# A two-layer trunk on one core: activation sums made a block ahead, own buffers for decay rows, and other places for the first weights

## The chip, the core and the metric

The kernel runs on one core of one Trainium2 chip. Its engines work side by side, each on a queue of its own and in the queue's order: TensorE (PE) multiplies into eight accumulator banks, VectorE (DVE) and ScalarE (ACT) work element by element, GpSimd (POOL) does a few small steps and issues some transfers, and SyncE (SP) issues the transfers of weights. The metric is the time of one execution on the device in microseconds (us).

## The reference

The input x has 256 tokens of width 2048, in float32. Layer 0 multiplies the normed x with one wide matrix (l0_w_in), whose columns feed an mLSTM group (q, k, v, output gate o, gates i and f) and a state-space group (z, x, B, C, dt); both results go side by side through l0_w_out. Layer 1 is causal attention with 16 heads and rotary positions; with 256 tokens, one block is all there is. Each layer ends with a gated feed-forward network (FFN) of inner width 5632. Cut to its core:

```python
for layer in range(2):
    xn = rms_norm(x, norm_mix[layer])
    if layer == 0:
        q, k, v, o, ig, fg, z, xbc, dt = split(xn @ w_in)
        hm = rms_norm(mlstm_chunkwise(q, k, v, ig, fg)) * sigmoid(o)
        xs, bm, cm = split(silu(causal_depthwise_conv(xbc)))
        y = ssd_chunked(xs, dt, a, bm, cm) + ssd_d * xs
        y = rms_norm_by_group(y * silu(z))
        x = x + concatenate([hm, y]) @ w_out
    else:
        x = x + moba_attention(rope(q), rope(k), v) @ w_o     # q, k, v = split(xn @ w_qkv)
    xn = rms_norm(x, norm_ffn[layer])
    x = x + (silu(xn @ w_gate) * (xn @ w_up)) @ w_down
out = rms_norm(x, final_norm)
```

## The kernel before

**Numbers in two parts.** Each float32 operand is split into a high part in a reduced format (the cast, on ACT: names ending in h, such as wh) and the low rest (a subtraction on DVE: wl). A product is three matmuls: high by high, high by low, low by high. So each weight tile costs a transfer into `raw`, an ACT cast (L410, in the projections L335) and a DVE subtraction (L412, L336) before PE can use it.

**Units.** In the z block, l0_w_out, the FFN and l1_w_o, `block` works on two strips of 512 columns at a time and goes through the depth of 2048 in eight units of 256 rows. A unit is of kind P, plain, with 24 matmuls of 128x512, or of kind S, summed: a Strassen-like step with 21 matmuls, that multiplies sums of weight tiles (`sums`, L419 to L423, on DVE) with sums of activation tiles (`skx`). PLAN_X is "PSPSPSPP", PLAN_LATE "PPPSPSPP", PLAN_O "PPPPPSPP". An S unit adds into four banks acc_f and four banks acc_e; behind the last S unit the four acc_e are added up (`pre`, L475 to L479). Most blocks come in two halves (q = 0 and 1) of two strips each.

**Sums of activations.** `sums_of(kt, j)` (L293 to L300) makes one set: xg, high plus low part (L299), four combinations sf (L283 to L286), then the split of sf into skx: an ACT cast (L196) and a DVE subtraction (L197). `block` asks for them at most three units ahead of their use, within its own half. Sets live in three buffers, tag `small`.

**Turns.** Activations must lie with the depth on the partitions, so results are turned by PE (p_tr, L253), four 128x128 pieces into a bank, and then split by ACT and DVE (L196 and L197, or L199 and L200 with gains), in `turned`. `later(wait, ...)` puts a turn, or another small step, a number of units behind. The split of a turn is marked with a priority of 1200, which lets the scheduler place it ahead of other work on ACT and DVE.

**Order.** Each engine executes its instructions in the order in which the scheduler put them; a waiting instruction holds up everything behind it on that engine.

**Stages.** The first 529 us hold the projections of layer 0 by strips (`lin_w`, `lin_a`: accumulators acc_w, acc_a), with the gates at 110 to 135 us. In between stand mLSTM heads and state-space heads; each needs decay rows: `decay_rows` has POOL issue two transfers from a scratch tensor (L654), and DVE adds masks to them (L658). Their buffer is the one `rows`, or one of four `ba`, which the mLSTM also uses. From 532 us the z block runs, in two halves; behind each, y is gated: thz (ACT L914, DVE L915), y (DVE L916), sums of squares (ACT L505), rs (DVE L191), rrg (POOL L192), y again (ACT L925), for four 128x512 pieces. From 640 us l0_w_out multiplies the mLSTM part (`mixed`, tiles mx) in two halves, and from 742 us the state-space part (`gated`, tiles my). Then the first FFN (to 1540), q, k, v and attention in four groups (to 1835), l1_w_o (`add_blocks` on oT) and the second FFN.

**Start of the kernel.** The sums of squares of x (ACT L505) write their squares into a temporary buffer; from them the norm is made (`row_norm`: dg on DVE L315, p_rb on PE L316). The gate weights wg come by POOL's queue and are cast by ACT (L196).

**Banks.** `ring["acc"]` is (0, 1, 2, 3, 4, 5); accumulators are taken in turn. In the last attention group (g = 3), the values' acc_a are set to start at bank 4, which the keys' strip used last.

Of the kernel before, what the change touches and what calls it, by code (L numbers as in the profile page):

```python
# [17 lines left out]
P = 128  # L18
# [23 lines left out]
STAGING = {"raw": 3, "wh": 3, "wl": 3}  # L42
MIXER = ({"raw": 4, "wh": 3, "wl": 3}, {"cb": 1}, {"rows": 1}, {"gap": 12288}, {"hm": 2}, {"gap": 192}, {"ba": 4}, {"cols": 2},
         {"wide": 2})
# [21 lines left out]
def hybrid_trunk(ctx: ExitStack, tc: tile.TileContext, a: dict, out: bass.AP):  # L66
# [42 lines left out]
    def open_staging():  # L109

        close_stage()
        for guard, pool, tags in open_pool("st", (STAGING,)):
            ctx.callback(guard.__exit__, None, None, None)
            staging.append((pool, tags))

    def held_tile(tag, shape, name, dt=F32):
# [3 lines left out]
        raise KeyError(tag)  # L120

# [125 lines left out]
    def transpose_split(kt, b, src, gcol, half):  # L247
# [6 lines left out]
        with tc.high_priority(offset=1200):  # L254
            turned(kt, b, pt.rearrange("p (a b) -> p a b", a=2), gcol, half)
# [65 lines left out]
    def chunks(w, col, nk, first=KC):  # L321

        n = 4 if staging else KC
        for k in range(0, nk, KC):
            if k % n == 0:
                raw = held_tile("raw", [P, n, STRIP], "raw")
                wh = held_tile("wh", [P, n, STRIP], "wh", F32R)
                wl = held_tile("wl", [P, n, STRIP], "wl", F32R)
# [65 lines left out]
    def weights(src, row, summed):  # L394

        def unit(kind, name, dt=F32):
            turn[kind] = turn.get(kind, -1) + 1
            spare = kind == "raw" and turn[kind] % 4 == 3
            return held_tile("rawx" if spare and stage["spare"] else kind, [P, 4, STRIP], name, dt)

        raw = unit("raw", "raw")
# [4 lines left out]
        def parts(of, cuts):  # L406
            h = unit("wh", "wh", F32R)
            l = unit("wl", "wl", F32R)
# [6 lines left out]
        with tc.high_priority(offset=800):  # L415
            if not summed:
                return parts(raw, (slice(0, 2), slice(2, 4)))
            sums = unit("raw", "sums")
# [6 lines left out]
    def block(src, kt, row, nk, plan, after_sums=None, lead=1, pairs=None):  # L425
# [21 lines left out]
        for i_, j in enumerate(order):  # L447
            for i in range(i_, min(i_ + 3, n)):
# [54 lines left out]
    def sumsq(acc, src):  # L503
        j = t2([P, src.shape[-1]], "sq")
# [25 lines left out]
    for c in range(4):  # L530
        for t in range(NT):
            sumsq(ss0[:, t, c:c + 1], xin[t][:, c * STRIP:(c + 1) * STRIP])
# [263 lines left out]
    def ssd_half(s, half):  # L796
        need("cb")
        h0 = 8 * s + 4 * half
        srows = decay_rows(MH + h0, slot_b if s > 1 and half else slot_a)
# [50 lines left out]
    def add_blocks(w, kt, row, nk, plans, finish=None, begin=None, whole=None, pairs=None):  # L850

        for q in range(2):
# [11 lines left out]
            F, _ = block(((w, c0), (w, c0 + STRIP)), kt, row, nk, plans[q], add_all, 2 if final else 1, pairs and list(pairs))  # L864
# [282 lines left out]
```

## Time and profile before

| what | value |
|---|---|
| runs | 2668.72, 2671.80 and 2671.93 us, median 2671.8 us |
| profiled execution | 2667.37 us, its span 2665.5 us |
| PE, DVE, ACT busy | 97%, 82%, 54% of the span |
| granted clock of PE, mean | 0.99 |
| HBM read | 492.39 MB, 186 GB/s over the span |

A row of the waits says which engine and line waited, for whom, for how long in total, how many times, and the longest. A row of stretches gives the busy time of each engine between two points, and the clock that PE was granted. A row of the order of time gives start, length, engine, line, operation, and in brackets how long the engine had been idle and what ended that.

### The profile page before, as it was taken

Reading aid. Unit: us, or ns where it says so; the run is one execution under the profiler, and the core shown is the slowest. Engines: PE = TensorE matmul, PEld = TensorE weight load, DVE = VectorE, ACT = ScalarE, POOL = GpSimd, SP = SyncE. Lnnn points to the kernel's source line nnn. Section 1 sums busy time; section 2 is a strip of 40 time slices with the busy share of each in tenths; the row PEclk is TensorE's granted clock in tenths of the full one; section 3 lists DMA queues with packets and bytes.
Section 4 is the critical chain, followed back from the end, with each engine's and each line's share of the span. In section 5 each row is a group of like instructions: output and inputs, shape, how many; then the busy total and the mean of one; then the engine's idle time right before and its main releaser. Section 6 shows DMA issues by size and latency. Waiting matters only on the chain.

```text
span 2665.5 us, 32524 instructions
## 1 busy us (share of the span) xinstructions
PE 2595.1 (97%) x12201; PEld 2137.3 (80%) x12201; DVE 2172.7 (82%) x2784; ACT 1442.8 (54%) x1916; POOL 46.0 (2%) x81
## 2 busy tenths in 40 slices
PE   8999999988999999999999999999999999999997
PEld 7888878866878777878787888887787788778876
DVE  5676777788999998889889975665899888988897
ACT  5465655556556555455445555555565545554544
POOL 2000010000000000000000000000000000000000
PEclk9999999998999999999999999999999999999999
DMA  7566576453656466556655655554546565566564
GB/s 215 169 190 197 165 218 186 143 197 127 221 170 216 159 210 215 177 187 200 211 190 190 196 184 183 177 173 131 189 167 213 173 214 182 197 199 196 190 199 140
DMA packets 254767, 496.68 MB, mean 186 GB/s; under 512 B 15704, under 2 KB 16608, under 8 KB 254352
## 3 DMA queue, kind: packets, MB, share of 16 engines
q1 hardware_dynamic: 250528, 483.52, 55.8%
q0 software_dynamic: 2896, 8.51, 1.1%
q10 hardware_dynamic: 1184, 2.56, 0.3%
q8 instruction: 96, 1.57, 0.2%
q14 instruction: 63, 0.52, 0.1%
HBM read 492.39 MB, written 2.14 MB: 186 GB/s over the span
## 4 chain that ended last, share of the span: by engine, by line
PE 86%; DVE 7%; ACT 3%; DMA 2%; issue 2%; POOL 0%; SPq 0%; DVEq 0%; POOLq 0%; ACTq 0%
PE acc_f L441 16%; PE acc_f L442 16%; PE acc_f L440 15%; PE acc_w L351 10%; PE acc_w L355 5%; PE acc_e L441 3%; PE acc_e L440 3%; PE acc_e L442 3%; PE acc_a L378 3%; PE acc_a L380 3%; PE acc_a L379 3%; DVE wl L412 3%; ACT wh L410 1%; PE p_tr L253 1%; PE p_y L823 1%
## 5 line engine op out<-in xcount | busy, mean ns | idle before, releaser
L410 ACT CAST wh<-raw 128x1024 fp32r<-128x1024 f32 (+1 forms) x548 | 599.7, 1135 | 443.8 <-PE acc_f L442 319.9
L412 DVE TENSOR_TENSOR wl<-raw,wh 128x1024 fp32r<-128x1024 f32 (+1 forms) x548 | 713.3, 1325 | 129.6 <-ACT wh L410 126.5
L336 DVE TENSOR_TENSOR wl<-raw,wh 128x1024 fp32r<-128x1024 f32 (+1 forms) x257 | 309.0, 1218 | 175.5 <-ACT wh L335 174.7
L441 PE MATMUL acc_f<-wl,x 128*128 128x512 f32 x1024 | 401.0, 392 | 0.5
L440 PE MATMUL acc_f<-wh,x 128*128 128x512 f32 x1024 | 399.9, 392 | 0.0
L442 PE MATMUL acc_f<-wh,x 128*128 128x512 f32 x1024 | 399.3, 390 | 0.0
L335 ACT CAST wh<-raw 128x1024 fp32r<-128x1024 f32 (+1 forms) x257 | 264.0, 1046 | 223.8 <-PE acc_w L351 134.8
L410 ACT CAST wh<-sums 128x1024 fp32r<-128x1024 f32 x216 | 221.6, 1048 | 184.0 <-PE acc_f L442 91.1
L412 DVE TENSOR_TENSOR wl<-sums,wh 128x1024 fp32r<-128x1024 f32 x216 | 259.0, 1220 | 12.1 <-ACT wh L410 11.9
L441 PEld LDWEIGHTS acc_f<-wl,x 128*128 128x128 f32 x1024 | 192.3, 188 | 43.2 <-DVE wl L412 2.7
L440 PEld LDWEIGHTS acc_f<-wh,x 128*128 128x128 f32 x1024 | 192.3, 188 | 43.1 <-ACT wh L410 4.1
L442 PEld LDWEIGHTS acc_f<-wh,x 128*128 128x128 f32 x1024 | 192.3, 188 | 39.2
L351 PE MATMUL acc_w<-xa,wh 128*128 128x512 f32 x768 | 211.0, 403 | 1.6 <-ACT wh L335 1.6
L351 PEld LDWEIGHTS acc_w<-xa,wh 128*128 128x128 f32 x768 | 140.6, 191 | 28.3 <-ACT wh L335 2.0
L351 PE MATMUL acc_w<-x,wh 128*128 128x512 f32 x512 | 138.6, 399 | 0.0
L419 DVE TENSOR_TENSOR sums<-raw 128x1024 f32<-128x1024 f32 x108 | 131.8, 1220 | 5.0 <-DMA raw<-in_l_ffn_up 2.5
L355 PE MATMUL acc_w<-xa,wl 128*128 128x256 f32 x768 | 122.4, 284 | 0.0
L355 PEld LDWEIGHTS acc_w<-xa,wl 128*128 128x128 f32 x768 | 111.1, 192 | 6.9
L441 PE MATMUL acc_f<-wl,ha 128*128 128x512 f32 x280 | 109.5, 393 | 1.2 <-DVE wl L412 0.9
L441 PE MATMUL acc_f<-wl,hb 128*128 128x512 f32 x280 | 109.7, 393 | 0.9 <-DVE wl L412 0.6
L442 PE MATMUL acc_f<-wh,hb 128*128 128x512 f32 x280 | 108.7, 389 | 0.0
L442 PE MATMUL acc_f<-wh,ha 128*128 128x512 f32 x280 | 108.5, 389 | 0.0
(363 smaller groups left out, 4750.0 us busy)
## 6 DMA issues: line engine op xcount, KB each, us to landing
raw<-in_l_w_in SPq DMA_DIRECT2D x191, 512.0 KB, 3.8
raw<-in_l_ffn_gate SPq DMA_DIRECT2D x176, 512.0 KB, 3.9
raw<-in_l_ffn_up SPq DMA_DIRECT2D x176, 512.0 KB, 4.9
raw<-in_l_ffn_down SPq DMA_DIRECT2D x176, 512.0 KB, 5.1
raw<-in_l_w_qkv SPq DMA_DIRECT2D x96, 512.0 KB, 4.5
raw<-in_l_w_out SPq DMA_DIRECT2D x64, 512.0 KB, 5.2
raw<-in_l_w_o SPq DMA_DIRECT2D x32, 512.0 KB, 4.9
rows<-scr POOLq DMA_DIRECT2D x10, 512.0 KB, 5.6
```

Of the source, the lines that this page charges most:

```text
L335: nc.scalar.copy(wh[:, ks, :], raw[:, ks, :])
L336: nc.vector.tensor_sub(wl[:, ks, :], raw[:, ks, :], wh[:, ks, :].bitcast(F32))
L351: nc.tensor.matmul(banks[f], wh[:, kk, f * P:(f + 1) * P], kt.both(k0 + kk), start=k0 + kk == 0, stop=False, skip_group_check=True)
L355: nc.tensor.matmul(banks[f][:, :T], wl[:, kk, f * P:(f + 1) * P], kt.parts(k0 + kk)[0], start=False, stop=k0 + kk == nk - 1, skip_group_ch ...
L378: nc.tensor.matmul(banks[t], xh[:, ts], wh[:, kk, :], start=k0 + kk == 0, stop=False)
L379: nc.tensor.matmul(banks[t], xh[:, ts], wl[:, kk, :], start=False, stop=False)
L410: nc.scalar.copy(h[:, c, :], of[:, c, :])
L412: nc.vector.tensor_sub(l[:, c, :], of[:, c, :], h[:, c, :].bitcast(F32))
L419: nc.vector.tensor_sub(sums[:, 0:2, :], raw[:, 2:4, :], raw[:, 3:0:-2, :])
L440: nc.tensor.matmul(dst, ah, bh, start=start, stop=False)
L441: nc.tensor.matmul(dst, ah, bl, start=False, stop=False)
L442: nc.tensor.matmul(dst, al, bh, start=False, stop=stop)
```

## The change

It has seven pieces; the work done is the same, instruction for instruction, apart from where it stands and where its data lie.

1. `block` and `add_blocks` take a list `ahead`: sets of activation sums of the next half or the next block that are made at a given unit of this one. The z block's first half makes the set that its second half lacks; the second half makes the three of l0_w_out's `mixed`; the second half of `mixed` makes two of `gated`; l1_w_o's first half makes two of its second.
2. The decay rows have three buffers `rows` of their own, in place of one plus 12288 bytes of gap, and no longer use `ba`.
3. The staging buffers for weights are nine pools of one buffer each, in another order of addresses, so that the first unit of z lies over space that is free by then.
4. Only the turns for the normed x of later stages (x1, x2, x3) keep the priority of 1200; the turns of mixed, gated, oT and h have 0.
5. The last attention group takes its banks in the order 0, 1, 4, 5, 2, 3, from the first one.
6. The squares of x go into the tile kT, which is written later.
7. The norm for the rotary table comes one step later.

```diff
-STAGING = {"raw": 3, "wh": 3, "wl": 3}
-MIXER = ({"raw": 4, "wh": 3, "wl": 3}, {"cb": 1}, {"rows": 1}, {"gap": 12288}, {"hm": 2}, {"gap": 192}, {"ba": 4}, {"cols": 2},
-         {"wide": 2})
+STAGING = tuple({tag: 1} for tag in "raw1 raw2 wh1 wh2 wl1 raw0 wh0 wl0 wl2".split())
+MIXER = ({"raw": 4, "wh": 3, "wl": 3}, {"cb": 1}, {"rows": 3}, {"hm": 2}, {"gap": 192}, {"ba": 4}, {"cols": 2}, {"wide": 2})
...
+    def unit(kind, shape, name, dt=F32):
+
+        if not staging:
+            return held_tile(kind, shape, name, dt)
+        n = turn[kind] = turn.get(kind, -1) + 1
+        if kind == "raw" and stage["spare"]:
+            if n % 4 == 3:
+                return held_tile("rawx", shape, name, dt)
+            n -= n // 4
+        return held_tile(f"{kind}{n % 3}", shape, name, dt)
...
-        with tc.high_priority(offset=1200):
+        with tc.high_priority(offset=1200 if kt.name in ("x1", "x2", "x3") else 0):
             turned(kt, b, pt.rearrange("p (a b) -> p a b", a=2), gcol, half)
...
-    def block(src, kt, row, nk, plan, after_sums=None, lead=1, pairs=None):
+    def block(src, kt, row, nk, plan, after_sums=None, lead=1, pairs=None, ahead=()):
...
         for i_, j in enumerate(order):
+            for i, kt_, j_ in ahead:
+                if i == i_:
+                    sums_of(kt_, j_)
             for i in range(i_, min(i_ + 3, n)):
                 if plan[i] == "S" and order[i] not in kt.sums:
                     sums_of(kt, order[i])
...
-            sumsq(ss0[:, t, c:c + 1], xin[t][:, c * STRIP:(c + 1) * STRIP])
+            sumsq(ss0[:, t, c:c + 1], xin[t][:, c * STRIP:(c + 1) * STRIP], kT[:, 2 * c:2 * c + 2, :].rearrange("p a b -> p (a b)"))
...
-        srows = decay_rows(MH + h0, slot_b if s > 1 and half else slot_a)
+        srows = decay_rows(MH + h0, slot_b)
...
-        F, pre = block(tuple((w_in, C_Z + (s0 + n) * STRIP) for n in range(2)), xt0, 0, KD, PLAN_X if q else PLAN_LATE)
+        F, pre = block(tuple((w_in, C_Z + (s0 + n) * STRIP) for n in range(2)), xt0, 0, KD, PLAN_X if q else PLAN_LATE,
+                       ahead=((4, mixed, 1), (6, mixed, 3), (7, mixed, 5)) if q else ((4, xt0, 1),))
...
-    add_blocks(a["l0_w_out"], mixed, 0, KD, (PLAN_X, PLAN_X))
+    add_blocks(a["l0_w_out"], mixed, 0, KD, (PLAN_X, PLAN_X), ahead=((), ((2, gated, 3), (4, gated, 1))))
...
-    later(5, "rope", rope_norm)
+    later(6, "rope", rope_norm)
...
     for g in range(4):
+        if g == 3:
+            ring["acc"], turn["acc"] = (0, 1, 4, 5, 2, 3), 0
         q = rope_strip(g * STRIP, "q4")
         k = rope_strip(D + g * STRIP, "k4")
-        if g == 3:
-            turn["acc"] = 4
...
-    add_blocks(a["l1_w_o"], oT, 0, KD, (PLAN_O, PLAN_X), finish)
+    add_blocks(a["l1_w_o"], oT, 0, KD, (PLAN_O, PLAN_X), finish, ahead=(((6, oT, 1), (7, oT, 3)), ()))
```

The changed kernel's lines stand 10 to 13 further down: L299 is L309 there, L412 is L418, L916 is L928.

The order of DVE's instructions behind the first half of z, before (xa_148 is the first tile of the normed x, y_2730 and y_2731 the two token halves of y):

```order
L915 SCALAR_TENSOR_TENSOR thz<-thz,pre 128x512
L916 SCALAR_TENSOR_TENSOR y_2730<-thz,rh_426,y_2730 128x512
L191 TENSOR_SCALAR rs<-ssg 128x2
L915 SCALAR_TENSOR_TENSOR thz<-thz,pre 128x512
L916 SCALAR_TENSOR_TENSOR y_2731<-thz,rh_426,y_2731 128x512
L299 TENSOR_TENSOR xg<-xa_148 128x512
L191 TENSOR_SCALAR rs<-ssg 128x2
L283 TENSOR_TENSOR sf<-xg 128x128
```

and the same set of sums in the changed kernel, whose tile is named xa_144, in the first half of z:

```order
L309 TENSOR_TENSOR xg<-xa_252 128x512
L296 TENSOR_TENSOR sf<-xg,sf 128x128
L293 TENSOR_TENSOR sf<-xg 128x128
L294 TENSOR_TENSOR sf<-xg 128x128
L295 TENSOR_TENSOR sf<-sf,xg 128x128
L309 TENSOR_TENSOR xg<-xa_144 128x512
L207 TENSOR_TENSOR skx<-sf,skx 128x4x128
L418 TENSOR_TENSOR wl<-raw,wh 128x1024
```

The set has moved from behind the gating of y to the first half's own two sets.

DVE at the change from z to l0_w_out, before (mx_3802 and mx_4292 are tiles of `mixed`):

```order
L916 SCALAR_TENSOR_TENSOR y_2730<-thz,rh_426,y_2730 128x512
L191 TENSOR_SCALAR rs<-ssg 128x2
L915 SCALAR_TENSOR_TENSOR thz<-thz,pre 128x512
L916 SCALAR_TENSOR_TENSOR y_2731<-thz,rh_426,y_2731 128x512
L299 TENSOR_TENSOR xg<-mx_3802 128x512
L191 TENSOR_SCALAR rs<-ssg 128x2
```

and in the changed kernel (my_5772 is a tile of `gated`, whose turns are L210):

```order
L294 TENSOR_TENSOR sf<-xg 128x128
L295 TENSOR_TENSOR sf<-sf,xg 128x128
L210 SCALAR_TENSOR_TENSOR my_5772<-p_tr,pv,my_5772 128x256
L296 TENSOR_TENSOR sf<-xg,sf 128x128
L927 SCALAR_TENSOR_TENSOR thz<-thz,pre 128x512
L418 TENSOR_TENSOR wl<-raw,wh 128x1024 x2
L418 TENSOR_TENSOR wl<-raw,wh 128x1536
L207 TENSOR_TENSOR skx<-sf,skx 128x4x128 x2
L928 SCALAR_TENSOR_TENSOR y_2718<-thz,rh_414,y_2718 128x512
L210 SCALAR_TENSOR_TENSOR my_5772<-p_tr,pv,my_5772 128x256
```

The sums of `mixed` now stand ahead of the gating or behind its first step, and turns and weights stand among its steps.

PE in the last attention group, before (p_o is the previous heads' output, p_pt the turn of the probabilities, acc_a the values' accumulators):

```order
L1028 MATMUL p_qk<-k_14167,q_13933 128x128
L1029 MATMUL p_qk<-k_14167,q_13933 128x256
L1059 MATMUL p_o<-pT,v_14344 128x256
L1060 MATMUL p_o<-pT,v_14344 128x128
L1051 MATMUL p_pt<-ident,prob 128x128
L378 MATMUL acc_a<-wh,x_12269 128x512
```

and in the changed kernel, where p_o comes behind 12 matmuls of acc_a and p_pt behind 48:

```order
L1040 MATMUL p_qk<-k_14178,q_13944 128x128
L1041 MATMUL p_qk<-k_14178,q_13944 128x256
L388 MATMUL acc_a<-wh,x_12280 128x512
L389 MATMUL acc_a<-wl,x_12280 128x512
L390 MATMUL acc_a<-wh,x_12280 128x512
```

The turn of the probabilities no longer stands ahead of the values' matmuls.

More of the change, by code (lines that the diff above doesn't have):

```diff
@@ L111, in open_staging @@
         close_stage()
-        for guard, pool, tags in open_pool("st", (STAGING,)):
+        for guard, pool, tags in open_pool("st", STAGING):
             ctx.callback(guard.__exit__, None, None, None)
@@ L325, in chunks @@
             if k % n == 0:
-                raw = held_tile("raw", [P, n, STRIP], "raw")
-                wh = held_tile("wh", [P, n, STRIP], "wh", F32R)
-                wl = held_tile("wl", [P, n, STRIP], "wl", F32R)
+                raw = unit("raw", [P, n, STRIP], "raw")
+                wh = unit("wh", [P, n, STRIP], "wh", F32R)
+                wl = unit("wl", [P, n, STRIP], "wl", F32R)
             step = KC if k else first
@@ L394, in weights @@
     def weights(src, row, summed):
[L396 to L401, printed above, removed]
+        shape = [P, 4, STRIP]
+        raw = unit("raw", shape, "raw")
         for i, (w, col) in enumerate(src):
@@ L406, in parts @@
         def parts(of, cuts):
-            h = unit("wh", "wh", F32R)
-            l = unit("wl", "wl", F32R)
+            h = unit("wh", shape, "wh", F32R)
+            l = unit("wl", shape, "wl", F32R)
             for c in cuts:
@@ L417, in weights @@
                 return parts(raw, (slice(0, 2), slice(2, 4)))
-            sums = unit("raw", "sums")
+            sums = unit("raw", shape, "sums")
             nc.vector.tensor_sub(sums[:, 0:2, :], raw[:, 2:4, :], raw[:, 3:0:-2, :])
@@ L501, in block, with sumsq @@
         return F, pre
-    def sumsq(acc, src):
-        j = t2([P, src.shape[-1]], "sq")
+    def sumsq(acc, src, j=None):
+        j = t2([P, src.shape[-1]], "sq") if j is None else j
         nc.scalar.activation(j, src, AF.Square, accum_out=acc)
@@ L848, in col_norm, with add_blocks @@
         return r
-    def add_blocks(w, kt, row, nk, plans, finish=None, begin=None, whole=None, pairs=None):
+    def add_blocks(w, kt, row, nk, plans, finish=None, begin=None, whole=None, pairs=None, ahead=((), ())):
         for q in range(2):
@@ L863, in add_blocks @@
             final = q and whole is not None
-            F, _ = block(((w, c0), (w, c0 + STRIP)), kt, row, nk, plans[q], add_all, 2 if final else 1, pairs and list(pairs))
+            F, _ = block(((w, c0), (w, c0 + STRIP)), kt, row, nk, plans[q], add_all, 2 if final else 1, pairs and list(pairs),
+                         ahead[q])
             if final:
```

## The prediction

> **What bounds the kernel now.** I read the page's busy line first, then the waits of TensorE (PE), then a table of stretches around them, and last the order of time inside the long waits.
>
> ```profile
> span 2665.5 us, 32524 instructions
> PE 2595.1 (97%) x12201; PEld 2137.3 (80%) x12201; DVE 2172.7 (82%) x2784; ACT 1442.8 (54%) x1916; POOL 46.0 (2%) x81
> ```
>
> PE is the bound: it sits idle for 2665.5 − 2595.1 = 70.4 us, and its instructions stay the same in number and shape. Only that idle time, and the slow clock that goes with it, can be won. The waits of PE (total us, times, longest us) say whom it waits for:
>
> ```profile
> PE acc_f L440 <- ACT skx L196: 23.6, 4, 10.8
> PE p_pt L1051 <- ACT prob L1045: 6.6, 2, 6.5
> PE acc_e L440 <- ACT wh L410: 4.4, 8, 0.7
> PE p_rb L316 <- DVE dg L315: 4.4, 2, 3.6
> PE acc_f L440 <- ACT wh L410: 3.3, 2, 3.1
> PE p_xs L793 <- DVE xsT L754: 3.1, 1, 3.1
> ```
>
> The table of stretches (width, busy time of PE, PEld, DVE, ACT, POOL, then the granted clock) shows where they lie:
>
> ```profile
> 0.00:45.00 45.00, 35.61 (x181) 29.70 (x182) 25.78 (x45) 27.22 (x53) 14.47 (x36) 0.96 0.75 229
> 360.00:390.00 30.00, 25.71 (x119) 20.48 (x118) 20.98 (x41) 17.53 (x35) 2.13 (x3) 0.94 0.63 206
> 529.00:540.00 11.00, 6.50 (x22) 4.22 (x22) 10.61 (x22) 7.97 (x13) 0.00 (x0) 0.69 0.79 285
> 540.00:585.00 45.00, 45.00 (x200) 37.26 (x199) 37.59 (x39) 21.42 (x21) 0.00 (x0) 1.00 0.55 188
> 585.00:608.00 23.00, 13.36 (x53) 10.38 (x52) 15.14 (x25) 14.76 (x33) 3.15 (x4) 0.78 0.28 92
> 640.00:670.00 30.00, 18.77 (x70) 14.14 (x69) 24.24 (x43) 20.52 (x42) 2.76 (x4) 0.77 0.27 87
> 786.00:800.00 14.00, 12.89 (x56) 10.03 (x55) 10.65 (x15) 7.34 (x7) 0.00 (x0) 1.00 0.52 174
> 925.00:1540.00 615.00, 612.01 (x2693) 493.50 (x2693) 544.36 (x602) 323.90 (x346) 0.00 (x0) 1.00 0.59 194
> 1800.00:1830.00 30.00, 23.55 (x110) 19.64 (x109) 15.61 (x24) 12.79 (x24) 0.00 (x0) 0.89 0.33 106
> 1895.00:1910.00 15.00, 12.69 (x50) 9.89 (x49) 12.07 (x20) 6.63 (x8) 0.00 (x0) 0.89 0.35 112
> 1945.00:2560.00 615.00, 612.79 (x2700) 495.06 (x2698) 544.57 (x612) 318.26 (x334) 0.69 (x1) 1.00 0.59 194
> ```
>
> What a stretch loses I take as its idle time plus (1 − clock) × busy time. Without a stall the clock is 1.00 and a matmul takes 45.00/200 = 0.225 us. So 0–45 loses 9.39 + 1.4 = 10.8; 360–390 loses 5.8; 529–540, the start of the z block, 4.5 + 2.0 = 6.5; 585–608, its second half, 9.64 + 2.9 = 12.6; 640–670, the first half of the l0_w_out block, 11.23 + 4.3 = 15.5; 786–800 1.1; 1800–1830 6.45 + 2.6 = 9.0; 1895–1910 3.7; the two long FFN stretches 3.0 + 2.2 = 5.2.
>
> **The change part by part.** Only what a part's wait costs counts; the work is the same, in another order.
>
> *Sums a block ahead (z second half, l0_w_out, gated, l1_w_o).* The order of time around the wait at 591–601 (start, length, engine, work, in brackets the idle time before it):
>
> ```profile
> 593.18 0.69 POOL L192 TENSOR_TENSOR rrg<-rs,mhalf 128x2 f32<-128x2 f32 x1 [2.02 <-DVE rs L191]
> 593.54 0.69 DVE L915 SCALAR_TENSOR_TENSOR thz<-thz,pre 128x512 f32<-128x512 f32 x1 [0.44 <-ACT thz L914]
> 598.00 0.68 DVE L299 TENSOR_TENSOR xg<-xa 128x512 f32<-128x512 f32 x1
> 600.92 0.60 ACT L196 CAST skx<-sf 128x512 fp32r<-128x512 f32 x1
> 601.58 0.79 PE L440 MATMUL acc_f<-wh,skx 128*128 128x512 f32 x1 [9.64 <-ACT skx L196]
> ```
>
> The sum xg stands in DVE's queue behind four gating steps that pass from ACT to DVE to POOL and back, and PE waits 9.64 us for it. One set of sums is one xg (0.68), four sf and the low part, and the cast of 0.60 on ACT:
>
> ```profile
> L283 DVE TENSOR_TENSOR sf<-xg x30: 278/283/291, 531.3 to 2556.3; 128x128 f32<-128x128 f32 x30
> ```
>
> With 4 × 0.28 and another 0.68 that is about 2.5 us of DVE. That work now runs in the first half, where 540–585 shows 45.00 − 37.59 = 7.4 us of idle DVE: it fits. The gating steps remain, beside unit work whose weights still need DVE, so I do not take all 12.6 but 9 (bounds 3, if DVE passes two thirds of the delay on to the low weights, and 12.6).
>
> In l0_w_out three sets were made after the gating (15.5 lost); now one is made ahead of it and two behind its first step. But the first summed unit of the new block still needs weights whose buffers come free only when the previous block's last unit ends, and DVE has the sums, four additions to the accumulators and the turns of y to do there: by its own rows 24.24 busy of 30. Two 1024-wide low parts, one set of sums and one addition in a row are some 2 × 1.18 + 2.5 + 0.68 = 5.5 us that PE can overtake. I expect a wait of about 5, long enough to keep its slow clock (4.3): 15.5 − 5 − 4.3 = 6.2, taken as 6 (bounds −2, the wait stays and two turns of y come on top, and 15.5). In gated 1 of 1.1 (0 to 1.1); in l1_w_o 2.5 of 3.7 (1 to 3.7), since DVE is busy 12.07 of 15 there and may hand on part of the wait.
>
> A rule weighed here: the Trainium skill's "TensorE: Matmul & The Clock Gate" (Part 1) has the clock drop after at least one idle window of some 3.4 us and return after one busy one. The row 1895–1910 differs: 2.3 us idle in all, clock 0.89. By the page that stretch would lose 2.3 and not 3.7, and the sum would be some 1.4 smaller; by the row it stays.
>
> *First z weights in free space, turns at normal priority.* PE waited 3.1 us for wh at the start of z (the acc_f <- ACT wh row), since ACT's cast stood behind the last work of the strips. With the unit's three buffers in space that is free, transfer and cast come three places earlier, and the eight turns p_tr go behind the unit's 24 matmuls (24 × 0.225 = 5.4 us, which covers tho). I take 5 of 6.5 (2 to 6.5): 1.5 stays because DVE, 10.61 busy of 11, has the second unit's low weights late.
>
> *Three row buffers.*
>
> ```profile
> 135.63 1.57 POOL L654 DMA_DIRECT2D rows<-scr  x2 [1.69 <-PE acc_w L351]
> ...
> 359.25 1.49 POOL L654 DMA_DIRECT2D rows<-scr  x2 [12.92 <-PE p_num L701]
> DVE rows L658 <- DMA rows<-scr: 14.1, 11, 3.8
> rows<-scr POOLq DMA_DIRECT2D x10, 512.0 KB, 5.6
> ```
>
> The transfer at 359.25 waited for a buffer that p_num held; DVE then waited 3.8 us for it, and the 3.1 us of p_xs follow. With own buffers it is issued right behind the early set of 135.63. Of 5.8 lost I take 5 (bounds −3 and 5.8): three sets back to back at 5.6 us a transfer can make DVE wait some 3 us more than it does now around 145, and there only a strip's weight lead covers it.
>
> *Start.*
>
> ```profile
> 34.34 1.48 ACT L196 CAST wgh<-wg 128x1536 fp32r<-128x1536 f32 x1 [5.97 <-DMA wg<-in_l_w_in]
> 11.67 0.47 ACT L199 ACTIVATE xa<-p_tr,pv 128x256 fp32r<-128x256 f32 x1 [1.65 <-PE p_tr L253]
> L558 POOL DMA_DIRECT2D alog<-in_l_ssd_a_log x1: 528/528/528, 7.5 to 7.5; - x1
> ```
>
> The gate cast blocked ACT for 5.97 us and dg behind it (p_rb 3.6). It moves ten places down, and p_rb some 25 matmuls down: 3.6 and its 1.4 of clock come back, 5. Against it the ACT row lam comes up to the tenth place, and waits there for a transfer issued at 7.5; with 5.6 us of landing that is 13.1, against 11.67 when ACT next evacuates a turn now: 1.5 lost. Net 3.5 (1 to 5).
>
> *Bank order of the last attention group.*
>
> ```profile
> 1806.30 2.35 DVE L336 TENSOR_TENSOR wl<-raw,wh 128x1024 fp32r<-128x1024 f32 x2
> 1812.52 0.42 DVE L386 TENSOR_TENSOR rsrc<-acc_w,rsrc 128x256 f32<-128x256 f32 x1
> 1812.90 0.47 PE L1051 MATMUL p_pt<-ident,prob 128*128 128x128 f32 x1 [6.46 <-ACT prob L1045]
> 1813.03 0.77 PE L378 MATMUL acc_a<-wh,x 128*128 128x512 f32 x1
> ```
>
> The 6.46 are put down to prob, yet acc_a starts right behind the accumulator's release at 1812.52 too: two releases end together. Both are dealt with: four banks for acc_a are free, and p_pt goes behind 48 of its matmuls (48 × 0.225 = 10.8 us against 6.46). Weights are there at 1808.65 at the latest. I take 8 of 9.0 (4 to 9).
>
> *FFN and rope.* Six waits of 0.67 (acc_e <- wh) shrink, as wh<-sums comes half a microsecond earlier: 2 of 5.2 (−2 to 5.2). rope's norm goes one step back: 0.5 of p_rb's second wait, 4.4 − 3.6 = 0.8 (0 to 0.8).
>
> Sum: 3.5 + 5 + 5 + 9 + 6 + 1 + 2 + 0.5 + 8 + 2.5 = 42.5. The profiled execution took 2667.4 us, so it becomes 2624.9. The median of the runs, 2671.8, lies 4.4 above it, which I carry over: 2629.
>
> **The rivals.**
> *DVE is the bound from 529 to 830.* In 585–608 it is busy 15.14 of 23, so this stretch waits on a chain; but 529–540 has 10.61 of 11, and 640–670 24.24 of 30, so there its load itself may set the pace. Then the waits only change their name: z start, z second half, l0_w_out and gated give 4 instead of 21, FFN 0 instead of 2. 42.5 − 19 = 23.5 gained: 2648.
> *Everything comes back.* All caps: 5 + 5.8 + 6.5 + 12.6 + 15.5 + 1.1 + 5.2 + 0.8 + 9 + 3.7 = 65; with l0_w_out at 10 still 59.7: 2612. For it speaks that DVE has 18% idle; against it that no DVE work is removed.
> *Slower: late turns.* Turns of mixed, gated, oT and h lose their priority and stand behind weight casts. At eight block halves PE could meet such a turn a whole unit late: 8 × 5.4 = 43 plus the clock (some 2 each, as 585–608 lost 2.9) is 59, which outweighs 42.5: 2688. It decides from 42.5/8 = 5.3 us of lateness on average. In the FFN it cannot:
>
> ```profile
> L197 DVE TENSOR_TENSOR skh<-sf,skh x12: 683/684/686, 884.0 to 2560.6; 128x512 fp32r<-128x512 f32 x12
> L440 PE MATMUL acc_f<-wh,skh x24: 389/389/398, 1003.6 to 2637.0; 128*128 128x512 f32 x24
> ```
>
> The first sum of h is there 119 us before PE reads it, the last 76 us. For the other blocks the order puts the turns two to four rows of weights later (2.4 to 5 us), which their unit order mostly covers.
> *The change does not do what it says.* The new addresses of the first weights may still overlap used space; only the z start hangs on that: 5 less, 2634, inside the forecast.
>
> **How the numbers follow.** Forecast (2620 to 2640) 0.58, DVE as the bound 0.25, everything 0.10, slower 0.05, and 0.02 that every wait only moves and nothing is left. The range, 2611 to 2653, takes in the forecast, the full recovery and most of the DVE case. A measurement here tells some 0.2% (5.3 us) from no change: faster 0.58 + 0.25 + 0.10 = 0.93; of the slower case 0.01 ends within that bound, so same 0.03 and slower 0.04.
>
> **What would show it.** Right: 585–608 without the skx wait, 1800–1830 at clock 1.00 with acc_a ahead of p_pt, no p_xs wait at 375, DVE's longest wait for rows under 2 us, p_rb's wait gone, and a wait of some 5 us for wh, wl or a turn at the head of l0_w_out. Wrong: PE waits of over 5 us for wl or xa, my or p_tr in 585–830 (DVE the bound), a DVE wait for rows at 140–160 with PE idle behind it, ACT waiting for alog for more than 2 us, or a clock under 1.00 in the long FFN stretches.

## The result, and the profile after

The changed kernel took 2628.53 us in the median of four runs (2624.91 to 2630.45), the kernel before 2671.24 us beside it (2668.72 to 2671.93): a ratio of 0.984, with a 95% interval of 0.9823 to 0.9857. The forecast was 2629 us. The profiled execution of the changed kernel is the slowest of its four (2630.45 us, span 2628.7), and that of the kernel before lies below all its others (2667.37), so between the two profiles only 2665.5 − 2628.7 = 36.8 us of span are to be found, where the medians differ by 42.7.

The waits of PE in the changed kernel (total us, times, longest us; its lines stand 6 to 12 further down, L410 is L416, L440 is L447, L1051 is L1063):

```profile
PE p_tr L263 <- ACT pre L485: 4.9, 1, 4.9
PE acc_e L447 <- ACT wh L416: 3.2, 5, 1.2
PE p_tr L263 <- DVE pre L487: 2.9, 1, 2.9
PE p_rows L189 <- DMA ident<-in_ident: 2.9, 1, 2.9
PE acc_f L448 <- DVE wl L418: 2.5, 6, 1.1
PE acc_f L447 <- ACT skx L206: 2.4, 1, 2.4
...
PE p_tr L263 <- DVE pre L486: 1.3, 1, 1.3
```

The 23.6 us for skx are down to 2.4; the waits for prob, dg, xsT and the 3.1 us for wh are gone. New are the first, the third and the last of these rows: 9.1 us in which the turn of y (p_tr) waits for the copy and the sums of accumulators (pre), which still hold the banks that the turn needs. The forecast had expected one wait of some 5 us there, for wh, wl or a turn; no term of it named pre.

The table of stretches after. Everything stands earlier in time than before, so a stretch is not the same work, but the stalls can be found in it:

```profile
0.00:45.00 45.00, 38.76 (x210) 32.63 (x211) 25.60 (x46) 27.14 (x53) 14.09 (x36) 1.00 0.78 237
...
360.00:390.00 30.00, 29.99 (x160) 24.99 (x158) 28.01 (x54) 21.98 (x41) 3.02 (x4) 1.00 0.71 207
...
585.00:608.00 23.00, 18.13 (x81) 14.71 (x80) 20.23 (x26) 16.69 (x32) 3.88 (x4) 0.99 0.55 189
608.00:640.00 32.00, 29.26 (x118) 22.55 (x119) 28.94 (x50) 17.44 (x29) 1.38 (x2) 0.90 0.40 130
640.00:670.00 30.00, 26.36 (x108) 20.24 (x109) 25.64 (x31) 15.70 (x27) 0.69 (x1) 0.94 0.47 143
...
786.00:800.00 14.00, 14.00 (x75) 11.86 (x74) 13.93 (x28) 11.28 (x23) 0.00 (x0) 1.00 0.16 62
...
1800.00:1830.00 30.00, 29.95 (x145) 24.86 (x144) 21.36 (x40) 18.33 (x41) 0.00 (x0) 1.00 0.39 122
1830.00:1895.00 65.00, 62.56 (x279) 51.34 (x278) 55.33 (x71) 34.95 (x47) 0.00 (x0) 0.97 0.56 184
```

360 to 390 and 1800 to 1830 run through at clock 1.00. From 585 to 670 PE still stands idle for 4.87 + 2.74 + 3.64 = 11.3 us, and the clock falls to 0.90 and 0.94.

To see where the time went, one measure serves through the rest of this text. The **lead** at a place is how much earlier a matmul starts than the same matmul in the kernel before (the same one in number, counted among its kind from the start of the program). It can be read in any two rows that give first and last start of a group, here the groups of the big blocks, before:

```profile
L378 PE MATMUL acc_a<-wh,xa x256: 387/389/628, 138.5 to 529.1; 128*128 128x512 f32 x128
L440 PE MATMUL acc_f<-wh,xa x98: 389/389/796, 535.4 to 632.4; 128*128 128x512 f32 x98
L440 PE MATMUL acc_f<-wh,mx x92: 388/389/501, 633.1 to 731.8; 128*128 128x512 f32 x92
L440 PE MATMUL acc_f<-wh,my x98: 388/389/476, 732.5 to 821.4; 128*128 128x512 f32 x98
L440 PE MATMUL acc_f<-wh,o x104: 389/389/580, 1837.5 to 1934.4; 128*128 128x512 f32 x104
```

and after:

```profile
L388 PE MATMUL acc_a<-wh,xa x256: 387/389/478, 133.5 to 516.8; 128*128 128x512 f32 x128
L447 PE MATMUL acc_f<-wh,xa x98: 388/389/481, 517.5 to 602.2; 128*128 128x512 f32 x98
L447 PE MATMUL acc_f<-wh,mx x92: 388/389/735, 611.7 to 705.8; 128*128 128x512 f32 x92
L447 PE MATMUL acc_f<-wh,my x98: 389/389/476, 706.4 to 793.3; 128*128 128x512 f32 x98
L447 PE MATMUL acc_f<-wh,o x104: 388/389/580, 1798.7 to 1895.7; 128*128 128x512 f32 x104
```

The lead is 138.5 − 133.5 = 5.0 us at the first values, 12.3 at the last strip, 632.4 − 602.2 = 30.2 at z's last weights, but 21.4 at the first matmul of l0_w_out, 26.1 at the first of the gated part, 28.1 at its last, 38.8 at the start of l1_w_o and 38.7 at the end of that group. Between z and l0_w_out 9 us of what was won are lost again. With more places in between, all read from the two traces in the same way (the mixed part of l0_w_out is all that stands ahead of the gated part):

| place | forecast, us | lead there | won, us |
|---|---|---|---|
| start | 3.5 | 0 to 5.0 | 5.0 |
| decay rows | 5 | 5.0 to 12.2 | 7.2 |
| z start | 5 | 12.2 to 18.8 | 6.5 |
| z second half and l0_w_out's mixed part | 9 + 6 | 18.8 to 26.1 | 7.3 |
| gated | 1 | 26.1 to 28.1 | 2.1 |
| both FFN and the end | 2 | 28.1 to 29.4, 37.7 to 38.8, 36.8 at the end | 0.5 |
| rope | 0.5 | 29.4 to 30.4 | 1.0 |
| attention | 8 | 30.4 to 38.8 | 8.4 |
| l1_w_o | 2.5 | 38.8 to 37.7 | −1.1 |
| sum | 42.5 | | 36.9 |

### The profile page after: what moved, and what is told of

Same layout as the page of the kernel before. It is cut to its first block, busy times and chain, and to the rows that moved or that the text cites. A ratio compares the mean times of both kernels' runs of the same rounds, so it can differ in the third digit from the quotient of the medians.

```text
span 2628.7 us, 32556 instructions
## 1 busy us (share of the span) xinstructions
PE 2589.4 (99%) x12201; PEld 2134.0 (81%) x12201; DVE 2170.1 (83%) x2784; ACT 1439.2 (55%) x1916; POOL 46.2 (2%) x81
## 4 chain that ended last, share of the span: by engine, by line
PE 87%; DVE 6%; DMA 2%; ACT 2%; issue 2%; POOL 0%; SPq 0%; DVEq 0%; POOLq 0%; ACTq 0%
PE acc_f L448 16%; PE acc_f L449 16%; PE acc_f L447 16%; PE acc_w L361 10%; PE acc_w L365 5%; PE acc_e L448 3%; PE acc_e L449 3%; PE acc_a L389 3%; PE acc_a L388 3%; PE acc_a L390 3%; PE acc_e L447 3%; DVE wl L418 3%; ACT wh L416 1%; PE p_tr L263 1%; PE p_y L833 1%
## 5 line engine op out<-in xcount | busy, mean ns | idle before, releaser
L416 ACT CAST wh<-raw 128x1024 fp32r<-128x1024 f32 (+1 forms) x548 | 599.8, 1135 | 439.7 <-PE acc_f L449 289.2
L418 DVE TENSOR_TENSOR wl<-raw,wh 128x1024 fp32r<-128x1024 f32 (+1 forms) x548 | 712.5, 1324 | 116.6 <-ACT wh L416 114.3
L447 PE MATMUL acc_f<-wh,x 128*128 128x512 f32 x1024 | 401.6, 392 | 0.1
L416 ACT CAST wh<-sums 128x1024 fp32r<-128x1024 f32 x216 | 221.2, 1048 | 164.3 <-PE acc_f L449 84.4
L418 DVE TENSOR_TENSOR wl<-sums,wh 128x1024 fp32r<-128x1024 f32 x216 | 258.5, 1218 | 9.5 <-ACT wh L416 9.2
L447 PEld LDWEIGHTS acc_f<-wh,x 128*128 128x128 f32 x1024 | 192.3, 188 | 43.2 <-ACT wh L416 4.2
```

The source lines that it names most:

```text
L416: nc.scalar.copy(h[:, c, :], of[:, c, :])
L418: nc.vector.tensor_sub(l[:, c, :], of[:, c, :], h[:, c, :].bitcast(F32))
L447: nc.tensor.matmul(dst, ah, bh, start=start, stop=False)
```

## The experiments

All twelve runs have the changed kernel as their base. Each ran beside the kernel before on its own chip (2667.24, 2667.1 and 2666.69 us in the three sets), so runs are compared by their ratio and by their lead, not by their microseconds; the changed kernel did not run beside them, but its 0.984 is some 2624 us there. Six of the twelve are single executions, with a ratio but no interval: those without the list for l1_w_o, and with rows, banks, staging, squares and priority undone. Executions of one kernel lie up to 5.5 us apart (2624.91 to 2630.45 above), so these six are read by place, from the lead.

### Without the sums made ahead

```diff
-        F, pre = block(..., PLAN_X if q else PLAN_LATE,
-                       ahead=((4, mixed, 1), (6, mixed, 3), (7, mixed, 5)) if q else ((4, xt0, 1),))
+        F, pre = block(..., PLAN_X if q else PLAN_LATE)
-    add_blocks(a["l0_w_out"], mixed, 0, KD, (PLAN_X, PLAN_X), ahead=((), ((2, gated, 3), (4, gated, 1))))
+    add_blocks(a["l0_w_out"], mixed, 0, KD, (PLAN_X, PLAN_X))
-    add_blocks(a["l1_w_o"], oT, 0, KD, (PLAN_O, PLAN_X), finish, ahead=(((6, oT, 1), (7, oT, 3)), ()))
+    add_blocks(a["l1_w_o"], oT, 0, KD, (PLAN_O, PLAN_X), finish)
```

> The changed kernel with all four lists of sums made ahead taken out (z, mixed, gated, l1_w_o); everything else stays. In the changed kernel the lead over the kernel before (how much earlier the same matmul starts) went from 18.8 us at the end of z's first half to 26.1 behind the first half of l0_w_out, to 28.2 behind gated, and from 38.8 to 37.7 across l1_w_o. Theory A, the terms of the prediction stand (9 + 6 + 1 + 2.5) and only a new wait came on top: without the lists z and l0_w_out lose some 12 to 15 us, so about 2643 and a lead of 12 behind l0_w_out. Theory B, the lists moved the waits and kept half: without them the lead grows by 0 where it grew by 7.3, so about 2636 to 2638, and the waits of PE for skx come back (about 20 us in all) while those of p_tr for pre shrink. l1_w_o: by the prediction 2.5 us worse without its list, by the curve 1 us better.

Ratio 0.9894 (0.9877 to 0.991), 2638.1 us. The wait for skx is back:

```profile
PE acc_f L447 <- ACT skx L206: 23.4, 4, 12.3
```

Between the two matmuls that start at 586.0 and 709.2 us in the kernel before (from the first summed unit of z's second half to the second one of l0_w_out's second half; "the stretch" from here on), this run takes 123.5 us, the kernel before 123.1, the changed kernel 115.4. So the lists are worth 8 us there, and the list for gated 1.5 (the lead grows by 0.6 instead of 2.1). The lead behind l0_w_out's mixed part is 18.5 us, where theory A said 12 and theory B some 19. That is theory B: the lists removed 21 us of waits, and more than half of it went to other waits. The time as a whole does not part the theories: the ratio is 0.0054 above the changed kernel's, 14 us, as theory A had it, with some 4 us of uncertainty on either side, while the places account for 10 (12 if compared with the next run). At l1_w_o nothing came back: the lead grows by 1.3 without the list, where the changed kernel's fell by 1.1.

### Without the list for l1_w_o alone

```diff
-    add_blocks(a["l1_w_o"], oT, 0, KD, (PLAN_O, PLAN_X), finish, ahead=(((6, oT, 1), (7, oT, 3)), ()))
+    add_blocks(a["l1_w_o"], oT, 0, KD, (PLAN_O, PLAN_X), finish)
```

> The changed kernel without the two sets of sums of oT made ahead. Prediction: 2.5 us longer, the wait for skx at the head of l1_w_o's second half comes back (2.5 us) and the lead falls across that block by 4. Theory B, the wait was only moved (2.4 us for skx now stand in the first half, and 1.1 for wl in the second): the lead stays at 38.8 across the block, so 1 us shorter than the changed kernel, and 0 to 1 in all within the scatter of one profile.

2624.62 us against 2667.24: 0.984, as the changed kernel. The lead goes from 41.2 to 41.6 us across l1_w_o. The list did not even move the wait: it stands at the same matmul, the first for skx in the block's second half, in the kernel before and in the changed kernel:

```profile
1901.68 0.69 PE L440 MATMUL acc_f<-wh,skx 128*128 128x512 f32 x1 [2.31 <-ACT skx L196]
```

```profile
1862.98 0.50 PE L447 MATMUL acc_f<-wh,skx 128*128 128x512 f32 x1 [2.44 <-ACT skx L206]
```

and in this run, without the list, at 1860.03 with 2.07 us. Over all profiles the block wins −1.1 to +1.4 us with the list (without the run with the wait in the second FFN below) and 0.4 to 2.1 without it. What parts the profiles is not the list but the clock: behind this wait PE ran 3.4 us at half clock in eight of the thirteen profiles of changed kernels, and there the lead grows by −0.1 to 0.5 us up to the block's last weights; in the other five it grows by 1.6 to 1.9. Both groups hold runs with and without the list. So the list has no effect that these runs show, where 2.5 were forecast.

This run is of use for another reason: up to l1_w_o its code is that of the changed kernel, and yet its lead behind l0_w_out is 28.7, not 26.1. Over the five profiles whose code between z and gated is the changed kernel's (itself, this one, and those with rows, banks or squares undone), z's second half and l0_w_out's mixed part win 6.8 to 9.5 us together. So one profile's number for this stretch is good to some 2.5 us only, and the 7.3 of the table are at the low end.

### Gating of y as one piece

What stands between z and l0_w_out, in the changed kernel's order of time:

```profile
603.43 1.22 DVE L425 TENSOR_TENSOR sums<-raw 128x1024 f32<-128x1024 f32 x1 [0.26 <-DMA raw<-in_l_w_out]
...
604.57 1.98 ACT L416 CAST wh<-sums 128x1024 fp32r<-128x1024 f32 x2
...
606.45 0.90 ACT L937 ACTIVATE y<-y,rrg 128x256 f32<-128x256 f32 x2
607.26 0.56 ACT L485 COPY pre<-acc_e 128x512 f32<-128x512 f32 x1
607.88 1.11 PE L263 MATMUL p_tr<-ident,y 128*128 128x128 f32 x4 [4.87 <-ACT pre L485]
...
610.26 1.12 PE L263 MATMUL p_tr<-ident,y 128*128 128x128 f32 x4 [1.27 <-DVE pre L486]
```

In the kernel before the gating of the first half's y was over by 601, while PE stood and waited, and the turns of y came behind 24 matmuls of l0_w_out. Now PE runs on, the gating is spread among weight casts until 606.45, and ACT's copy of acc_e stands behind its last step. The turns of y now come ahead of l0_w_out on PE and need the accumulator banks that this copy releases. The run marks the gating with a priority, so that it stands ahead of the weights as one piece, as before:

```diff
         for n in range(2):
             ...
             for t in range(NT):
+                with tc.high_priority(offset=800):
                     th = t2([P, STRIP], "thz")
...
```

> The changed kernel, with the gating of y marked with a priority of 800, so that it stands as one piece on ACT and DVE ahead of the weights, and ACT's copy of acc_e (pre) behind z's second half no longer stands behind it. Theory A: PE's new waits at the change from z to l0_w_out (p_tr for pre, 4.9 + 1.3 + 2.9 us) come from the gating that is spread through the second half and stands ahead of that copy; then they vanish, the lead behind l0_w_out's first half rises from 26 to some 33 us, and the time falls to about 2621. Theory B: DVE's load is the bound from 585 to 700; then the waits come back as waits for skx, wl or wh of like size, the lead stays within 2 us of 26, and the time is 2628 within 3.

Ratio 0.984 (0.9825 to 0.9855), the changed kernel's. The waits of p_tr for pre are gone, and the stretch takes 114.2 us, where it took 115.4 (113.4 to 116.1 in the other runs with the same code there). In their place PE waits, between 566 and 684 us:

```profile
PE acc_e L447 <- ACT wh L416: 2.7, 2, 2.5
PE acc_f L447 <- ACT wh L416: 2.6, 3, 2.1
PE acc_f L448 <- DVE wl L418: 2.3, 4, 0.9
```

The lead behind l0_w_out's mixed part is 28.6 us, not theory A's 33 (theory B had 26 within 2). Theory A has fallen: the order of ACT's copy names the wait, it does not set the time.

### Fewer summed units in the stretch

```diff
-    add_blocks(a["l0_w_out"], mixed, 0, KD, (PLAN_X, PLAN_X), ahead=((), ((2, gated, 3), (4, gated, 1))))
+    add_blocks(a["l0_w_out"], mixed, 0, KD, (PLAN_LATE, PLAN_X), ahead=(((5, mixed, 1),), ((2, gated, 3), (4, gated, 1))))
...
-                       ahead=((4, mixed, 1), (6, mixed, 3), (7, mixed, 5)) if q else ((4, xt0, 1),))
+                       ahead=((6, mixed, 3), (7, mixed, 5)) if q else ((4, xt0, 1),))
```

> The changed kernel, with one summed unit of the first half of l0_w_out made a plain one (order of kinds PPPSPSPP in place of PSPSPSPP); its third set of sums is made at the sixth unit of that half, for the second. In the stretch of the second half of z and the first of l0_w_out, DVE's work is 105.5 us and PE's some 448 x 0.225 = 101 us. Theory A, DVE's load is the bound there: a summed unit costs DVE about 4 us more than a plain one, and the set of sums leaves the stretch (2.5 us), against 0.68 us more on PE: the stretch becomes 4 to 6 us shorter, the ratio to the kernel before about 0.982 where it was 0.984. Theory B, the order of a few instructions (the turns of y ahead of the block, ACT's copy of acc_e) sets the wait: DVE's load does not matter, and it gets 0 to 1 us longer.

The stretch takes 109.9 us, 5.5 less than in the changed kernel, with three matmuls more. But the ratio is 0.9853 (0.9838 to 0.9869), because 8 us are lost further on, at the start of the second FFN, where the code is unchanged: PE waits 5.0 us there for wh (the lead falls from 45.2 to 37.0). ACT's casts of the first FFN weights stand behind a whole turn of x in this run (from 1887.70), in the changed kernel two of them stand ahead of it (from 1889.36, with a lead that was 6.5 us smaller). Why the order came out so was not followed up.

With the second half of z of that kind as well:

```diff
-        F, pre = block(..., xt0, 0, KD, PLAN_X if q else PLAN_LATE,
-                       ahead=((6, mixed, 3), (7, mixed, 5)) if q else ((4, xt0, 1),))
+        F, pre = block(..., xt0, 0, KD, PLAN_LATE,
+                       ahead=((6, mixed, 3), (7, mixed, 5)) if q else ())
```

> As the run before, and the second half of z with PPPSPSPP as well, so that it needs no third set of sums. Theory A (DVE's load): DVE has some 13 us less to do in the stretch and PE 1.4 us more; then PE is the bound, the stretch gets 7 to 10 us shorter, the ratio about 0.981. Theory B: 0 to 2 us longer than the changed kernel.

Ratio 0.9814 (0.9797 to 0.9832), 2618.15 us: some 7 us below what the changed kernel's ratio gives there, though the two intervals overlap. The stretch of the same work in the kernel before, in the changed kernel, in the run with one plainer half and in this run (behind the width come the busy times of PE, PEld, DVE, ACT and POOL, then the clock):

```profile
586.00:709.20 123.20, 102.33 (x438) 82.78 (x437) 105.20 (x140) 73.12 (x114) 5.92 (x8) 0.90 0.47 155
```

```profile
567.30:682.70 115.40, 104.16 (x438) 82.22 (x436) 102.92 (x136) 70.06 (x113) 6.64 (x8) 0.96 0.50 164
```

```profile
566.70:676.60 109.90, 102.27 (x440) 82.05 (x439) 101.62 (x138) 70.08 (x114) 7.64 (x8) 0.97 0.51 173
```

```profile
567.00:674.90 107.90, 101.26 (x444) 80.91 (x443) 97.41 (x134) 67.63 (x112) 10.87 (x8) 1.00 0.49 165
```

In the changed kernel 438 matmuls of 0.225 us are 98.6 us of PE, and DVE has 102.9 us of work in the same stretch. However the queue stands, the stretch cannot be shorter than DVE's work; but it takes 115.4 us, so this floor is not reached, and DVE itself stands idle for 12.5 us of it. With two summed units fewer DVE has 97.4, PE six matmuls more, and the stretch loses 7.5 us. Theory A holds in its direction; its size does not follow from load alone, since the first of the two runs took only 1.3 us of DVE's work out (101.6) and won 5.5. Part of the size is the clock: PE's waits from 566 to 684 us shrink from 11.1 to 6.7 us, and the two times of half clock behind the longest of them, which cost the changed kernel some 4 us, are gone. In both runs the first summed unit also comes two units later, which gives DVE time behind the change of block. How much is load and how much that place, these two runs do not tell.

### Single parts undone

The row buffers:

```diff
-{"cb": 1}, {"rows": 3}, {"hm": 2},
+{"cb": 1}, {"rows": 1}, {"gap": 12288}, {"hm": 2},
...
-        srows = decay_rows(MH + h0, slot_b)
+        srows = decay_rows(MH + h0, slot_b if s > 1 and half else slot_a)
```

> The changed kernel with one row buffer, the gap and the use of ba again. If the row buffers are what won at 345 to 410 (the lead went from 4.2 to 12.2 us there): the DVE wait for rows of 3.8 us and the wait p_xs of 3 us come back and the lead stays at 5, 7 to 8 us longer; the loss of 0.5 at 135 to 156 in the changed kernel's profile goes. If the lead came from the other places of the work: less than 2 us change.

2632.24 us against 2667.1, 0.987. The lead stays at 5.6 where it went to 12.2: the buffers are worth 7. Both waits are back:

```profile
PE p_xs L803 <- DVE xsT L764: 3.1, 1, 3.1
...
DVE rows L668 <- DMA rows<-scr: 14.6, 11, 4.1
```

In the changed kernel DVE's row reads 6.7, 3, 3.0. The 0.5 us that its lead lost from 128 to 160 stand in no other run with three buffers but two (0.3 and 0.2), so they are not shown to be a price of the buffers.

The banks of the last attention group:

```diff
-        if g == 3:
-            ring["acc"], turn["acc"] = (0, 1, 4, 5, 2, 3), 0
         q = rope_strip(g * STRIP, "q4")
         k = rope_strip(D + g * STRIP, "k4")
+        if g == 3:
+            turn["acc"] = 4
```

> The changed kernel with the last attention group's banks as before. Prediction 8 us longer, all of it between 1795 and 1835, with the wait of p_pt for prob back at 6 to 7 us. Rival: the rope norm's step and the turns' priority have moved p_pt already, and less than 2 us come back.

2633.69 us, 0.9875. The lead falls from 31.7 to 30.6 from 1790 to 1835 us instead of rising by 8.3: the bank order is worth 8.3 to 9.4, and the wait is where it was:

```profile
PE p_pt L1063 <- ACT prob L1057: 6.5, 1, 6.5
```

The wait is as long as before; behind it PE ran 5.9 us at half clock here and 3.6 in the kernel before, and half of that difference is what parts 9.4 from 8.3.

The place of the first weights of z:

```diff
-STAGING = tuple({tag: 1} for tag in "raw1 raw2 wh1 wh2 wl1 raw0 wh0 wl0 wl2".split())
+STAGING = tuple({tag: 1} for tag in "raw0 raw1 raw2 wh0 wh1 wh2 wl0 wl1 wl2".split())
```

> The changed kernel with the nine staging buffers in the old order of addresses, so that z's first unit lies over space that is still in use. If the place of the first unit is what won at 527 to 546 (6.5 us), the wait for wh of about 3 us comes back and the lead there stays at 12 to 14 instead of 18.8. If the turns' later place alone won it, the lead is 18.8 all the same.

2633.67 us against 2666.69, 0.9876. The lead goes from 12.8 to 14.0 at the start of z instead of from 12.2 to 18.8, and the wait for wh is back (2.5 us): the place is worth 5.3 of the 6.5 us. Where the other 1.3 come from is not shown; it is not the turns' priority, since with that undone (below) the whole 6.5 stay. The time around z's start:

```profile
516.00:527.00 11.00, 7.32 (x27) 4.92 (x27) 10.39 (x21) 7.61 (x12) 0.00 (x0) 0.84 0.79 278
```

It lost 4.5 us of PE at 529 to 540 before, 3.7 here, and nothing in the changed kernel.

The squares of x:

```diff
-            sumsq(ss0[:, t, c:c + 1], xin[t][:, c * STRIP:(c + 1) * STRIP], kT[:, 2 * c:2 * c + 2, :].rearrange("p a b -> p (a b)"))
+            sumsq(ss0[:, t, c:c + 1], xin[t][:, c * STRIP:(c + 1) * STRIP])
```

> The changed kernel with the squares of x in the temporary buffer again. If that buffer's reuse tied the squares to other work, the wait of p_rb for dg (3.6 us) comes back and the lead at 50 us is 0 to 1 instead of 5. If the order of the gate cast alone won it, the lead is 5 all the same.

2626.55 us, 0.985. The lead at 52 us is 3.8 instead of 5.0, and p_rb does not wait. So the tile kT is worth some 1.2 us. The gate cast stands later without it as well (at 41.6 us, no longer waiting, where it was at 34.3 behind a wait of 5.97); that its place is the larger rest fits, but no run undoes it.

The turns' priority:

```diff
-        with tc.high_priority(offset=1200 if kt.name in ("x1", "x2", "x3") else 0):
+        with tc.high_priority(offset=1200):
```

> The changed kernel with all turns back at priority 1200. Theory A, the priority is what won the FFN term and lets the first weights of z go ahead: the lead no longer grows across the two FFN (2.4 us lost), z's start loses 3 to 5 us of its 6.5, so about 2634 to 2636. Theory B, the priority alone does nothing and the other pieces carry it: every stage within 1 us of the changed kernel, 2628 within 3.

2629.08 us against 2667.24, 0.9857. The lead at z's start is 19.0, the same: theory A fell for that part. Across the long stretch of the first FFN (925 to 1540 us before) it grows by 0.2 (0.8 in the changed kernel, 0.1 to 0.9 in the other runs), across that of the second by 0.4 (0.9, and 0.7 to 1.7 in the others). So the priority is worth at most some 1 us there, of which only the second FFN's half lies outside the scatter, and nothing else that shows.

### Combinations

No list for l1_w_o on top of the two plainer halves, and then the gating as one piece as well (edits as above):

> The two plainer halves of the run with both late, and no sums of oT ahead. If the two gains add (the first gave a ratio of 0.9814; without the oT list the changed kernel was some 1 us shorter), the ratio is about 0.981 and the lead across l1_w_o is kept or grows by 1; if the oT list was only scatter, the ratio equals that of the run with both late within 0.0005.

> As the run before, and the gating of y ahead as one piece. Theory A (DVE's load was the bound, and is no longer): now the order of single instructions counts, and the remaining waits at the head of l0_w_out (pre, xres: 4.3 us) shrink, 2 to 4 us shorter. Theory B (waits only trade places): the same within 1.5 us.

Ratios 0.9815 (0.98 to 0.9829) and 0.9811 (0.9794 to 0.9827), 2616.84 and 2615.86 us. Neither can be told from the run with both halves late (0.9814), so the two gains do not add, and of the second pair theory B holds: the waits for pre and xres are gone, and one of 3.1 us for wh stands in their place. The stretch takes 109.5 and 107.8 us, against 107.9. These three are the fastest of all, 49 to 51 us below the kernel before.

## Why the prediction was right, and where it was not

**The whole.** 42.5 us were forecast, 42.7 measured in the medians. That is closer than the steps deserve, and in part luck: the two profiles that the steps can be read from differ by 36.9, and the terms miss by −2.2 to +7.7 us each (forecast less won), in both directions. Over profiles of nearly the same code (the runs without the list for l1_w_o and with the squares in the old place) the lead at the end is 42.7 and 40.9.

**What bounds the kernel.** Right outside 585 to 700 us: where a single wait was taken away (rows, z's start, the banks, p_rb) the time of the wait and of its slow clock came back whole, and more than the terms had kept: 5.0 for 3.5, 7.2 for 5, 6.5 for 5, 8.4 for 8. Each was discounted for a new wait behind it, and the new waits cost little. DVE does wait 3.0 us for rows at 137 us, more than the 2 us that were to be a good sign, as the term's lower bound had it for three sets back to back; PE loses 0.5 us behind it. For the decay rows even the bound of 5.8 was too low: the stretch 360 to 390 left out what was lost outside it, 0.8 of it by 347 us.

**The start.** The cost of lam was worked out as waiting until 13.1; it starts at 13.20:

```profile
13.20 0.20 ACT L584 ACTIVATE lam<-alog 64x1 f32<-64x1 f32 x1 [3.27 <-DMA alog<-in_l_ssd_a_log]
```

The wait of 3.27 us was named as a sign of being wrong (over 2 us). But PE was behind by only 0.4 to 0.5 us at 8 to 30 us, not by 1.5, probably because it waits for x in that stretch anyway.

**z's second half and l0_w_out: the step that failed.** 9 + 6 = 15 were forecast, 7.3 came (6.8 to 9.5 over the profiles with the same code there). The waits for skx went in both places, as the step said. By place, the term for z came in full: the lead grows from 18.8 to 30.2 us up to z's last weights, 11.4 for 9. The term that failed is the one for l0_w_out, 6 with a lower bound of −2: there the lead falls from 30.2 to 26.1, −4.1. The step allowed for one wait of 5 us at its head with 4.3 of slow clock; in its place stood three waits for banks, 4.9, 1.3 and 2.9 us, with some 4 us of slow clock. How the sum divides hangs on the order of the gating (7.5 and 1.4 with the gating as one piece); the sum does not.

Behind it stands the argument that DVE's work fits because DVE has idle time in z's first half. The one set that moved there did leave the stretch (105.2 us of DVE's work became 102.9), but the gating and the weights, which DVE had done while PE stood still, were still to be done when PE ran on, and PE needs only 98.6 us. So waits came back under other names. That DVE's work there is the limit is borne out by three results: another order changes nothing (114.2 us), and less work shortens the stretch by 5.5 and 7.5. It is not shown to be the whole cause, since the first summed unit moved in the same two runs. This was the first rival, and it holds for this stretch alone, at about half its price: it put the loss at 17 us over z start, z, l0_w_out and gated, and the start of z and gated lost nothing. Its sign, a PE wait of over 5 us for p_tr, was missed by 0.1.

**gated and rope** gave 2.1 and 1.0 for 1 and 0.5. **l1_w_o** gave −1.1 (0.4 without the list) for 2.5. The step that failed there is that the list would put the sums ahead of the wait: the wait stands at the same matmul, 2.4 us where it was 2.3, and the lead is lost behind it, at a wait of 1.1 us for wl with the first FFN weights. **FFN**: 1.3 and 1.1 us between the places of the table, for the forecast's 2; the end lost 1.9. There, behind two waits of 1.2 and 0.7 us for the last down weights, PE runs 3.4 us at half clock (from 2604.2), which it does not in the kernel before. Other profiles with the same order of instructions there win or lose −2.5 to +2 at the end, so that is scatter.

**Late turns**, the slower rival, did not come: the turns of y into my do wait (9.1 us), but for banks, and not for their own splits; with priority 1200 the waits are no shorter, under the name of acc_e (7.5) and p_tr (3.5).

**The clock.** The first estimate of a stretch's loss, idle time plus (1 − clock) × busy time, holds where the slow clock lies behind the wait: 1830 to 1895 has one wait of 2.4 us and a clock of 0.97, 1.9 us more. The Trainium skill's "TensorE: Matmul & The Clock Gate" (Part 1) has the clock drop after at least one idle window of some 3.4 us. The traces do not agree: that wait of 2.4 us, and the one of 2.3 from 1895 to 1910 before, are shorter, and the clock dropped to 0.50 behind both. For long waits the estimate is too high, because the clock falls while PE still stands: in the kernel before it is 0.50 from 594.6 us on, PE runs again only at 601.6, and the clock is back at 604.7. Only the 3.2 us in which PE ran at half clock count, which cost 1.6 us where 2.9 were reckoned; in l0_w_out it ran 5.2 us so (657.5 to 662.8), which cost 2.6 where 4.3 were. The stretch lost 123.2 − 98.6 = 24.6 us before, not the 12.6 + 15.5 = 28.1 from which the two terms were taken.

## What to carry to other kernels

Before work is moved ahead of a wait, add up each engine's work over the whole stretch between the last and the next place where it has slack: where a second engine's work there exceeds the bounding engine's, part of what is moved comes back as waits under other names (here about half), and the next gain came from giving that engine less (a plain unit for a summed one), not from another order. Where the busy times leave room, a wait that was removed came back whole, with its slow clock. Read the gain by place, from the same matmul in both traces; a total that fits can hide terms that miss in both directions, and a wait that is thought to have moved can turn out to stand at the same matmul.

## What the runs showed of the hardware that was not expected

The same wait is not always followed by the slow clock. At l1_w_o PE waits 1.9 to 2.4 us for skx at the same matmul in all profiles. Behind it the clock was 0.50 for 3.4 us in the changed kernel and seven other runs, and 1.00 in five, here the run with the gating as one piece (a wait of 2.00 us) and the one without the list for l1_w_o (2.07 us):

```profile
1861.30:1864.30 3.00, 3.00 (x8) 2.32 (x7) 1.10 (x2) 2.06 (x5) 0.00 (x0) 0.50 0.00 0
```

```profile
1860.10:1863.40 3.30, 3.30 (x15) 2.69 (x16) 1.80 (x4) 2.37 (x3) 0.00 (x0) 1.00 0.01 4
```

Half the clock for 3.4 us is 1.7 us, and that is most of what parts one profile from another at l1_w_o. The three profiles that lose 1.6 to 2.5 us at the end have such a time of half clock there as well. What decides it, no run here shows.

The same code also gave 6.8 to 9.5 us over z's second half and l0_w_out. DVE's wait there for l0_w_out's weights was shortest (3.1 us) where most was won and 5.0 and 5.4 us where least was; whether it is the cause is not shown. Differences of 2.5 us are about half of what lies between executions of one kernel, so such a place is settled by several profiles and not by one.
